# Splitting one chunk ahead of the mix, and both retention directions in one product: the output stage of a hybrid layer

## The chip, the cores and the metric

One NeuronCore of a Trainium2 chip runs the whole layer as one program. The metric is the device time of one execution in microseconds (us); several executions are timed and the median is given. One further execution is taken with the hardware profiler; all rows below are from that one.

## What is computed

The reference is one layer of a diffusion transformer on 2048 tokens of width 1024 (and 256 context tokens): a modulated RMS norm, a token mix, a residual, a second norm, and a mixture of 16 experts. The token mix has two halves of 512 columns, retention and RWKV-7, each run forward and backward over the sequence. For the retention half (8 heads of 64, chunks of 128 tokens) the part that matters here is

```python
def head_rms(y):
    y = y * lax.rsqrt(jnp.mean(y * y, axis=-1, keepdims=True) + NORM_EPS)
...
decay_in = where(rel >= 0, exp(max(rel, 0) * log_gamma), 0)
q_dec = exp((idx + 1) * log_gamma)
scores = einsum('bhid,bhjd->bhij', qc, kc) * decay_in
out = einsum('bhij,bhjd->bhid', scores, vc) + einsum('bhid,bhde->bhie', qc * q_dec, S)
S = S * chunk_dec + einsum('bhjd,bhje->bhde', kc * k_dec, vc)
...
lat = silu(gf) * head_rms(y_f) + silu(gb) * head_rms(flip(y_b))
...
lat = concatenate([ret_lat, rwkv_lat]) @ w_out
x = x + gt1 * rms_norm(mix, g_post_mix)
```

Then come the router's logits from the second norm of x, the choice of 256 tokens for each expert, and the experts.

## The kernel before, in words

Three earlier stages write projected columns, the retention states and the RWKV outputs to DRAM. `out_phase` (from L1375) is the output stage; it takes a chunk of 128 tokens at a time, 16 chunks, and ends with the router's logits; the experts follow. Its parts for one chunk are methods of `Chunk`:

- `turns`: load q and k, 8 TensorE transposes into two PSUM tiles `pb`, two ScalarE copies to `qT` and `kT`.
- `scores`: `qds` = qT times a table of decays `qd` for both directions (one GpSimd pass of 1024 columns); two `pb` tiles of k times q (4 matmuls each), each multiplied on VectorE by the decay mask `rm` into an `sm` tile of 1024 columns (both directions).
- `loads`, `gates`: DMA loads of v and gates (`vg`), the backward state (`Sb`), the RWKV outputs (`ys`), bonus (`bon`) and gates (`gs`); then three GpSimd passes on `gs` and `bon`.
- `wkv`: square, reduce, root, reciprocal and scale of `ys` (the head norm), then times `gs`, plus `bon`, into the right half of `lat`.
- `outputs(d)`, once for each direction: 16 small matmuls of `qds` with the state into PSUM tile `py`, 16 of `sm` with v on top, a ScalarE copy to `yr`, square, reduce; root, reciprocal, scale, times gate. The second direction adds both into the left half of `lat`.
- `split`: 8 transposes of `lat` into two `pb` tiles; ScalarE rounds each into `lh`, VectorE writes the rest into `ll`.
- `mix`: 48 matmuls of 512 columns (lh and ll with the split weights) into two PSUM tiles `pm`. `mixed`: squares and row sums of `pm` on ScalarE, `h` = `pm` times a gain row on VectorE, root and reciprocal.
- `norms`: x + norm (`xt<-h` in the rows, two instructions), its squares, root, `h` = the second norm (VectorE), plus a shift row (GpSimd); stores. `route`: 8 transposes of x into two `pb` tiles, copies to `hT`, 8 matmuls of 16 columns into a `pb` tile, logits.

The loop over i (L1652) interleaves these by hand. In the round of i it does the mix of chunk i, `norms` and `route` of chunk i-1, `outputs` and `wkv` of chunk i+1, `scores` of i+2 and `turns` of i+3, and `split` of i+1 near its end, ahead of the last 8 matmuls of the mix. TensorE, VectorE, ScalarE and GpSimd keep the program's order each (`keep_in_program_order`, L126, which is why all rows show L126); DMA issues on SyncE are put in order by a planner. At the head of a round stand, in this order: `gates`; squares and reduce of `wkv`; x and its squares; the second norm; root and scale of `wkv`. Then come five steps of 8 mix matmuls each with the other parts between them.

The stage divides PSUM into eight tiles of 512 columns (banks): three for tiles named `pb`, three for `pm`, two for `py`. A `pb` tile is free when its last reader is done.

Of the kernel before, what the change touches and what calls it, by code (L numbers as in the profile page):

```python
# [35 lines left out]
def constants():  # L36
# [28 lines left out]
    qd = lambda e: np.exp(e[None, None, :] * chan[:, :, None]) / 8  # L65
    c["ret_qdec"] = np.stack([qd(i + 1), qd(128 - i)], 1).reshape(128, 1024).astype(f)
# [18 lines left out]
def body(ctx: ExitStack, tc, a, out, scratch, stop=None, only=None):  # L85
# [1289 lines left out]
    def out_phase():  # L1375
        with ExitStack() as es:
# [12 lines left out]
            qd = one.tile([128, 2, 512], F32, name="qd")  # L1389
# [58 lines left out]
            def squares(x, n):  # L1448

                sq = one.tile([128, HD * n], F32, name="sq%d" % n)  # L1450
                act.activation(sq, x, AF.Square)
                ss = two.tile([128, n], F32, name="ss%d" % n)
                vec.tensor_reduce(ss, heads(sq), axis=AX.X, op=OP.add)
                return ss

            def head_norm(x, ss, n, eps):

                rstd(ss, 1.0 / HD, eps)
                vec.tensor_mul(heads(x), heads(x), ss[:, :, None].to_broadcast([128, n, HD]))
# [10 lines left out]
            Sf = one.tile([128, 4, HD], F32, name="Sf", bufs=3)  # L1470
            nc.sync.dma_start(out=Sf.rearrange("p s e -> p (s e)"), in_=g.kvf[16])
            Sf = advance(Sf, 17)

            class Chunk:
# [5 lines left out]
                def turns(self):  # L1480
# [3 lines left out]
                    for j, n in enumerate(("qT", "kT")):  # L1484
# [3 lines left out]
                        t = one.tile([128, 4, 128], F32, name=n)  # L1488
# [17 lines left out]
                def loads(self):  # L1506
# [3 lines left out]
                    Sb = two.tile([128, 4, HD], F32, name="Sb")  # L1510
                    nc.sync.dma_start(out=Sb.rearrange("p s e -> p (s e)"), in_=g.rb[self.i])
# [6 lines left out]
                    self.parts = (u, Sb, ys, bon, gs)  # L1518

                def outputs(self, d, Sf):  # L1520

                    u, Sb = self.parts[:2]
                    S = Sb if d else Sf
                    py = pps.tile([128, 2, 512], F32, name="py", bufs=1)
                    pyv = py[:, :, 0:256].rearrange("p z (s d) -> p z s d", d=HD)
# [8 lines left out]
                    for s in range(4):  # L1534
                        for hh in range(2):
                            for th in range(2):
                                mm(pyv[H[th], hh, s, :], self.sm[hh][:, d, s, ts[th]], u[:, hc(2 * s + hh)],
                                   start=False, stop=(s == 3), skip_group_check=True)
                    yr = one.tile([128, W], F32, name="yr", bufs=2)
                    act.copy(out=yr.rearrange("p (s z d) -> p z s d", z=2, d=HD), in_=pyv)  # L1540
# [4 lines left out]
                    if d == 0:  # L1545
                        self.y0 = yr
                    else:
                        vec.tensor_add(self.lat[:, 0:W], yr, self.y0)
# [10 lines left out]
                def wkv(self):  # L1559

                    _, _, ys, bon, gs = self.parts
                    self.lat = one.tile([128, D], F32, name="lat")
                    y = ys.rearrange("p d n -> p (d n)")
                    ss = squares(y, 16)
                    yield
                    head_norm(y, ss, 16, gn_eps)
                    yield
# [5 lines left out]
                def split(self):  # L1573
                    self.lh = lh = two.tile([128, KT, 128], F32R, name="lh")
                    self.ll = ll = two.tile([128, KT, 128], F32R, name="ll")
                    for j in (1, 0):
# [5 lines left out]
                        vec.tensor_sub(ll[:, js], ps, lh[:, js].bitcast(F32))  # L1582

# [66 lines left out]
            nc.sync.dma_start(out=qd.rearrange("p d n -> p (d n)"), in_=a["c_ret_qdec"])  # L1650
            nc.sync.dma_start(out=rm.rearrange("p d z s t -> p (d z s t)"), in_=a["c_ret_mask"])
            for i in range(-2, NT + 1):  # L1652
                if i == -1:
                    nc.sync.dma_start(out=lnw, in_=bcast(a["rwkv_lnx_w"], W))
                outs, other = [none, none], none
# [7 lines left out]
                if on(i + 1):  # L1663
                    ch[i + 1].gates()
# [499 lines left out]
```

## Time and profile before

| What | Value |
|---|---|
| Median of 3 runs | 3589.23 us (3582.62 to 3590.91) |
| The profiled execution: its own time, its span | 3576.91 us, 3574.9 us |
| TensorE, VectorE, ScalarE, GpSimd busy over the span | 89%, 64%, 39%, 34% |
| Mean granted TensorE clock over the span | 0.935 |
| The stretch of 12 rounds, 1919.7 to 2245.0 us: TensorE, VectorE, ScalarE, GpSimd busy | 285.2, 251.0, 121.9, 145.4 us of 325.3 |
| The same stretch: granted clock | 0.91 |
| Its start, 1848 to 1885.6 us (before the first mix): TensorE busy, clock | 19.8 us of 37.6, 0.50 |

Times of rows are us from the start of the span unless marked ns. PE is TensorE, DVE VectorE, ACT ScalarE, POOL GpSimd, SP SyncE. `out<-in` are the program's tile names; xN after a row is the number of instructions merged into it. Ends of matmuls are modelled, so the distance from one start to the next is the better price. A granted clock of 1.00 is 2.4 GHz, 0.50 is 1.2 GHz.

### The profile page before, as it was taken

To read this page: it belongs to the slowest core of one execution; us is meant where nothing else is said; L and a number is where in the kernel's file an instruction comes from. 1 tells how busy PE (TensorE), PEld (TensorE's weight loads), DVE (VectorE), ACT (ScalarE), POOL (GpSimd) and SP (SyncE) were. 2 spreads that over 40 slices of the span, in tenths; PEclk is the share of its full clock that TensorE was granted. 3 is DMA by queue.
4 is the path that set the end of the run, shared out by engine and by line. 5 is a ranking of instruction groups with operands and counts; after the bars stand their busy time and mean duration, and the time that the engine had idled before them with its cause. 6 is when DMAs were issued, how large, how long until landed. Compare 5 with 4: busy or idle time off the path is not lost. (4 is left out here: it accounts for less than half of the span.)

```text
span 3574.9 us, 74834 instructions
## 1 busy us (share of the span) xinstructions
PE 3197.0 (89%) x30786; PEld 2783.1 (78%) x30786; DVE 2271.5 (64%) x3904; ACT 1380.3 (39%) x2468; POOL 1216.9 (34%) x1969
## 2 busy tenths in 40 slices
PE   6999999788888888999978888849999999998888
PEld 4898889666767777777766777639999999998787
DVE  6676745566657556546427777675655665567765
ACT  4645343222222223333333333324444444444443
POOL 2010101464554554453634444220000000017774
PEclk9999999888999999999978988869999999999999
DMA  8886763545445456455457544236766666678885
GB/s 259 258 250 197 220 191 119 177 147 163 151 146 181 149 180 195 145 167 168 159 187 245 184 164 163 91 118 212 224 199 211 214 204 207 204 233 302 284 297 192
DMA packets 468221, 692.80 MB, mean 194 GB/s; under 512 B 30232, under 2 KB 345253, under 8 KB 457001
## 3 DMA queue, kind: packets, MB, share of 16 engines
q1 hardware_dynamic: 441480, 550.62, 47.4%
q0 software_dynamic: 25824, 136.36, 12.5%
q8 instruction: 242, 3.96, 0.4%
q10 hardware_dynamic: 576, 1.05, 0.1%
q14 instruction: 99, 0.80, 0.1%
HBM read 534.56 MB, written 153.37 MB: 192 GB/s over the span
## 5 line engine op out<-in xcount | busy, mean ns | idle before, releaser
L126 DVE TENSOR_TENSOR ewl<-ewr,ewh 128x1024 fp32r<-128x1024 f32 x376 | 474.3, 1303 | 250.2 <-ACT ewh L126 250.2
L126 PE MATMUL pr<-rwh,rh 128*128 128x512 f32 x1344 | 484.6, 428 | 35.7 <-ACT ru L126 16.9
L126 ACT CAST ewh<-ewr 128x1024 fp32r<-128x1024 f32 x376 | 374.2, 1046 | 0.5 <-DMA ewr<-in_w_down_dram 0.5
L126 PEld LDWEIGHTS pr<-rwh,rh 128*128 128x128 f32 x1344 | 268.7, 202 | 101.9 <-ACT ru L126 18.6
L126 PE MATMUL pu<-hi,whi 128*128 128x258 f32 (+1 forms) x1104 | 327.2, 296 | 5.0 <-ACT hi L406 5.0
L126 PE MATMUL pu<-lo,whi 128*128 128x258 f32 (+1 forms) x1104 | 315.9, 286 | 4.0 <-DVE lo L407 2.3
L126 PE MATMUL pu<-hi,wlo 128*128 128x258 f32 (+1 forms) x1104 | 314.4, 285 | 0.0
L997 POOL TENSOR_TENSOR dtmp<-xp,dm 128x126 f32<-128x126 f32 (+22 forms) x558 | 248.1, 445 | 186.8 <-DVE xp L126 146.9
L126 PE MATMUL pg<-xh,ewh 128*128 128x256 f32 x1024 | 293.0, 286 | 0.0
L126 PE MATMUL pu<-xh,ewh 128*128 128x256 f32 x1024 | 289.9, 283 | 0.8 <-DVE sg L126 0.8
L126 PE MATMUL pg<-xh,ewl 128*128 128x256 f32 x1024 | 290.4, 284 | 0.0
L126 PE MATMUL pg<-xl,ewh 128*128 128x256 f32 x1024 | 290.3, 284 | 0.0
L126 PE MATMUL pu<-xl,ewh 128*128 128x256 f32 x1024 | 289.9, 283 | 0.0
L126 PE MATMUL pu<-xh,ewl 128*128 128x256 f32 x1024 | 289.8, 283 | 0.0
L126 PE MATMUL pr<-rwl,rh 128*128 128x512 f32 x672 | 282.4, 420 | 4.4 <-DVE rwl L126 4.4
L1000 POOL TENSOR_TENSOR dm<-dm,dtmp 128x126 f32<-128x126 f32 (+22 forms) x558 | 269.0, 482 | 43.0
L126 PEld LDWEIGHTS pu<-hi,whi 128*128 128x128 f32 (+1 forms) x1104 | 208.2, 189 | 14.6 <-ACT hi L406 5.8
L126 PE MATMUL po<-ewh,hh 128*128 128x512 f32 x512 | 212.2, 414 | 0.0
L126 PEld LDWEIGHTS pu<-lo,whi 128*128 128x128 f32 (+1 forms) x1104 | 208.0, 188 | 5.2 <-DVE lo L407 3.2
L126 PEld LDWEIGHTS pu<-hi,wlo 128*128 128x128 f32 (+1 forms) x1104 | 208.6, 189 | 2.8 <-issue 2.2
L126 PE MATMUL po<-ewh,hl 128*128 128x512 f32 x512 | 203.6, 398 | 0.0
L126 PE MATMUL po<-ewl,hh 128*128 128x512 f32 x512 | 202.9, 396 | 0.0
(525 smaller groups left out, 7720.0 us busy)
## 6 DMA issues: line engine op xcount, KB each, us to landing
rh<-s_hT POOLq DMA_DIRECT2D x84, 1024.0 KB, 6.0
ewr<-in_w_gate_dram SPq DMA_DIRECT2D x64, 1024.0 KB
ewr<-in_w_up_dram SPq DMA_DIRECT2D x64, 1024.0 KB
ewr<-in_w_down_dram SPq DMA_DIRECT2D x64, 1024.0 KB
s_ret<-ru SPq DMA_DIRECT2D x84, 256.0 KB
wraw<-in_w_in_dram SPq DMA_DIRECT2D x156, 128.0 KB
bk<-s_bk SPq DMA_DIRECT2D x17, 1024.0 KB
mw<-in_w_mod_dram SPq DMA_DIRECT2D x128, 128.0 KB
```

The lines of the kernel that those rows point to most:

```text
L126: return lambda *args, **kw: tc.keep_in_program_order(op(*args, **kw))
L997: x = eng.tensor_mul(tv, ma[:, j, 0:j, None].to_broadcast(sh), dm[:, j:j + 1, j // 2:].to_broadcast(sh))
L1000: eng.tensor_add(dm[:, 0:j, j // 2:], dm[:, 0:j, j // 2:], tv)
```

## The change

- The decay of the queries is taken out of the product: the state is multiplied with plain `qT`, and the mask `rm` now holds decays relative to that, exp(-(j+1) log gamma) and its mirror, without the factor 1/8. The head norm divides the common factor out again, since it is the same for a whole row of a head; only the epsilon has to be scaled, and a table `ret_eps` (16 numbers a token, tile `reps`) is added to the sums of squares. `qds` and its table are gone, and `qT` gets a second buffer.
- Forward and backward state lie in one tile `S` (three buffers). `outputs` runs once for both directions: 16 matmuls of 128 columns instead of 2 x 16 of 64, the same 32 with `sm`, and then one square, reduce, root, reciprocal, scale and gating over 1024 columns instead of two each over 512.
- `outputs`, `wkv`, `gates` and `loads` work on chunk i+2 in the round of i, `scores` on i+3, `turns` on i+4. `split` stays with chunk i+1, and its two halves move from the end of the round to behind the first 8 and the second 8 mix matmuls. The loop begins at -3 instead of -2.

```diff
-    dec = lambda r: np.where(r[:, None, :] >= 0, np.exp(np.maximum(r, 0)[:, None, :] * lg[order][None, :, None]), 0) / 8
-    c["ret_mask"] = np.stack([dec(rel[:, :]), dec(-rel)], 1).reshape(128, 2048).astype(f)
+    dec = lambda r, e: np.where(r[:, None, :] >= 0, np.exp(-e[:, None, None] * lg[order][None, :, None]), 0)
+    c["ret_mask"] = np.stack([dec(rel, i + 1), dec(-rel, 128 - i)], 1).reshape(128, 2048).astype(f)
...
-    c["ret_qdec"] = np.stack([qd(i + 1), qd(128 - i)], 1).reshape(128, 1024).astype(f)
+    ep = lambda e: EPS * 64 * 64 * np.exp(-2 * e[:, None] * lg[None, :])
+    c["ret_eps"] = np.stack([ep(i + 1), ep(128 - i)], 1).reshape(128, 16).astype(f)
...
-                n = one.tile([128, 4, HD], F32, name="Sf", bufs=3)
-                pool.tensor_mul(n, S, cdec)
-                pool.tensor_add(n, n, f)
+                n = one.tile([128, 2, 4, HD], F32, name="S", bufs=3)
+                pool.tensor_mul(n[:, 0], S[:, 0], cdec)
+                pool.tensor_add(n[:, 0], n[:, 0], f)
...
-                    self.qds = two.tile([128, 2, 4, 128], F32, name="qds")
-                    pool.tensor_mul(self.qds.rearrange("p d s t -> p d (s t)"),
-                                         qT.rearrange("p s t -> p (s t)")[:, None, :].to_broadcast([128, 2, 512]), qd)
...
-                    nc.sync.dma_start(out=Sb.rearrange("p s e -> p (s e)"), in_=g.rb[self.i])
+                    nc.sync.dma_start(out=S[:, 1].rearrange("p s e -> p (s e)"), in_=g.rb[self.i])
...
-                py = pps.tile([128, 2, 512], F32, name="py", bufs=1)
+                py = pps.tile([128, 2, 4, 2, HD], F32, name="py", bufs=1)
...
-                            mm(pyv[H[th], hh, s, :], self.qds[H[hh], d, s, ts[th]], S[H[hh], s, :],
+                            mm(py[H[th], hh, s], self.T[0][H[hh], s, ts[th]], S[H[hh], :, s, :],
                                start=(s == 0), stop=False, skip_group_check=True)
                 yield
...
-                ss = squares(yr, 8)
+                    yr = one.tile([128, 2 * W], F32, name="yr")
+                    for hh in range(2):
+                        act.copy(out=yr.rearrange("p (d s z e) -> p z s d e", d=2, z=2, e=HD)[:, hh], in_=py[:, hh])
+                    ss = squares(yr, "r")
+                    vec.tensor_add(ss, ss, reps)
                     yield
-                head_norm(yr, ss, 8, eps1)
-                vec.tensor_mul(yr, yr, u[:, W + W * d:2 * W + W * d])
+                    head_norm(yr, ss)
+                    yield
+                    vec.tensor_mul(yr, yr, u[:, W:3 * W])
+                    vec.tensor_add(self.lat[:, 0:W], yr[:, 0:W], yr[:, W:2 * W])
...
-            for i in range(-2, NT + 1):
+            for i in range(-3, NT + 1):
...
-                if on(i + 1):
-                    ch[i + 1].loads()
-                    outs = [ch[i + 1].outputs(d, Sf) for d in range(2)]
-                    other = ch[i + 1].wkv()
+                if on(i + 2):
+                    ch[i + 2].loads(S)
+                    outs, other = ch[i + 2].outputs(), ch[i + 2].wkv()
+                split = ch[i + 1].split() if on(i + 1) else none
...
                     for _ in range(8):
                         next(mix, None)
+                    if step < 2:
+                        next(split, None)
                     if step < 4:
-                        next(outs[step // 2], None)
+                        next(outs, None)
                     if step == 1:
-                        if on(i + 2):
-                            ch[i + 2].scores()
-                        next(outs[0], None)
+                        if on(i + 3):
+                            ch[i + 3].scores()
                         next(other, None)
...
-                if on(i + 3):
-                    ch[i + 3].turns()
-                if on(i + 1):
-                    ch[i + 1].split()
+                if on(i + 4):
+                    ch[i + 4].turns()
                 for _ in range(8):
                     next(mix, None)
```

## Rows read from the trace of the kernel before

**Rows 1.** Instructions of tile h: duration ns min/median/max, first and last start.
```profile
L126 DVE SCALAR_TENSOR_TENSOR xt<-h,s__21977,xt x2: 742/744/746, 1919.7 to 1920.3; 128x512 f32<-128x512 f32 x2
...
L126 DVE SCALAR_TENSOR_TENSOR xt<-h,s__25133,xt x2: 743/744/746, 2245.0 to 2245.7; 128x512 f32<-128x512 f32 x2
...
L126 DVE SCALAR_TENSOR_TENSOR xt<-h,s__25606,xt x2: 747/750/753, 2296.9 to 2297.5; 128x512 f32<-128x512 f32 x2
L126 DVE SCALAR_TENSOR_TENSOR xt<-h,s__25716,xt x2: 746/749/752, 2314.2 to 2314.9; 128x512 f32<-128x512 f32 x2
```

**Rows 2.** Timeline of PE in one round: start, length, instruction, [idle before <-releaser].
```profile
2049.52 0.39 PE L126 MATMUL pm<-woh,lh 128*128 128x512 f32 x1
...
2051.48 0.70 PE L126 MATMUL py<-Sf,qds 64*64 64x64 f32 x32
...
2054.17 1.15 PE L126 MATMUL py<-vg,sm 128*64 128x64 f32 x32
2055.25 1.71 PE L126 MATMUL pb<-qT,kT 64*128 64x128 f32 x16
...
2070.66 1.12 PE L126 MATMUL pb<-ident,lat 128*128 128x128 f32 x4 [2.03 <-ACT qT L126]
2072.70 1.09 PE L126 MATMUL pb<-ident,lat 128*128 128x128 f32 x4 [0.91 <-DVE lat L126]
...
2076.65 0.39 PE L126 MATMUL pm<-woh,lh 128*128 128x512 f32 x1
```

**Rows 3.** PE by stretches: length, busy (instructions), granted clock, DMA share, GB/s.
```profile
2069.20:2076.20 7.00, 4.62 (x15) 0.51 0.92 325
```

**Rows 4.** Timeline of PE in the second round.
```profile
1919.21 0.69 PE L126 MATMUL py<-Sf,qds 64*64 64x64 f32 x32
...
1936.66 0.66 PE L126 MATMUL pb<-ident,lat 128*128 128x128 f32 x4 [0.65 <-ACT qT L126]
...
1938.69 0.63 PE L126 MATMUL pb<-ident,lat 128*128 128x128 f32 x4 [1.38 <-DVE lat L126]
...
1942.98 0.69 PE L126 MATMUL py<-Sf,qds 64*64 64x64 f32 x32
```

**Rows 5.** Timeline of DVE in the round of rows 2.
```profile
2050.49 0.69 DVE L126 TENSOR_TENSOR h<-pm,row_gt 128x512 f32<-128x512 f32 x1 [1.72 <-ACT junk L126]
...
2058.38 3.35 DVE L126 TENSOR_TENSOR ys<-ys,ss 128x1024 f32<-128x1024 f32 x1
...
2062.24 2.34 DVE L126 TENSOR_TENSOR sm<-pb,rm 128x1024 f32<-128x1024 f32 x2
...
2066.54 1.22 DVE L126 TENSOR_TENSOR ys<-ys,gs 128x1024 f32<-128x1024 f32 x1
...
2071.86 0.69 DVE L126 TENSOR_TENSOR lat<-yr 128x512 f32<-128x512 f32 x1
...
2072.61 0.68 DVE L126 TENSOR_TENSOR ll<-pb,lh 128x512 fp32r<-128x512 f32 x1
```

**Rows 6.** Timeline of POOL in the same round.
```profile
2058.26 2.38 POOL L126 TENSOR_TENSOR h<-h,row_sh 128x1024 f32<-128x1024 f32 x1 [7.86 <-DVE h L126]
2060.60 3.36 POOL L126 TENSOR_TENSOR qds<-qT,qd 128x1024 f32<-128x1024 f32 x1
...
2072.29 1.40 POOL L126 TENSOR_TENSOR both<-gs 128x512 f32<-128x512 f32 x1 [6.94 <-DMA gs<-s_g]
```

**Rows 7.** Timeline of ACT in the same round.
```profile
2051.49 1.04 ACT L126 ACTIVATE sq<-ys 128x1024 f32<-128x1024 f32 x1
```

**Rows 8.** Timeline of SP (DMA issues) in the same round.
```profile
2067.78 0.37 SPq L1517 DMA_DIRECT2D gs<-s_g  x1
```

**Rows 9.** Timeline of PE at the start of the stage.
```profile
1861.63 1.13 PE L126 MATMUL py<-Sf,qds 64*64 64x64 f32 x32
...
1880.58 1.09 PE L126 MATMUL pb<-ident,lat 128*128 128x128 f32 x4 [6.60 <-DVE lat L126]
...
1885.61 0.78 PE L126 MATMUL pm<-woh,lh 128*128 128x512 f32 x1
```

More of the change, by code (lines that the diff above doesn't have):

```diff
@@ L1388, in out_phase @@
             rm = one.tile([128, 2, 2, 4, 128], F32, name="rm")
-            qd = one.tile([128, 2, 512], F32, name="qd")
+            reps = one.tile([128, 16], F32, name="reps")
             rows = {n: one.tile([128, D], F32, name="row_" + n) for n in ("gt", "sh2", "sc2")}
@@ L1446, in out_phase, with squares, head_norm @@
             heads = lambda x: x.rearrange("p (h e) -> p h e", e=HD)
-            def squares(x, n):
-                sq = one.tile([128, HD * n], F32, name="sq%d" % n)
+            def squares(x, name):
+                sq = one.tile([128, 1024], F32, name="sq" + name)
                 act.activation(sq, x, AF.Square)
-                ss = two.tile([128, n], F32, name="ss%d" % n)
+                ss = two.tile([128, 16], F32, name="ss" + name)
                 vec.tensor_reduce(ss, heads(sq), axis=AX.X, op=OP.add)
                 return ss
-            def head_norm(x, ss, n, eps):
-                rstd(ss, 1.0 / HD, eps)
-                vec.tensor_mul(heads(x), heads(x), ss[:, :, None].to_broadcast([128, n, HD]))
+            def head_norm(x, ss, *eps):
+                act.activation(ss, ss, AF.Sqrt, scale=1.0 / HD, **(dict(bias=eps[0]) if eps else {}))
+                vec.reciprocal(ss, ss)
+                vec.tensor_mul(heads(x), heads(x), ss[:, :, None].to_broadcast([128, 16, HD]))
             def advance(S, i):
@@ L1464, in advance @@
                 nc.sync.dma_start(out=f.rearrange("p s e -> p (s e)"), in_=g.kvf[i])
[L1465 to L1472 removed]
+                n = one.tile([128, 2, 4, HD], F32, name="S", bufs=3)
+                pool.tensor_mul(n[:, 0], S[:, 0], cdec)
+                pool.tensor_add(n[:, 0], n[:, 0], f)
+                return n
+            S = one.tile([128, 2, 4, HD], F32, name="S", bufs=3)
+            nc.sync.dma_start(out=S[:, 0].rearrange("p s e -> p (s e)"), in_=g.kvf[16])
+            S = advance(S, 17)
             class Chunk:
@@ L1487, in turns @@
                             turn(ps[:, s, :], u[:, W * j + 128 * s:W * j + 128 * s + 128], ident)
-                        t = one.tile([128, 4, 128], F32, name=n)
+                        t = one.tile([128, 4, 128], F32, name=n, bufs=2 if j == 0 else 1)
                         act.copy(out=t, in_=ps)
@@ L1530, in outputs @@
                             for th in range(2):
-                                mm(pyv[H[th], hh, s, :], self.qds[H[hh], d, s, ts[th]], S[H[hh], s, :],
+                                mm(py[H[th], hh, s], self.T[0][H[hh], s, ts[th]], S[H[hh], :, s, :],
                                    start=(s == 0), stop=False, skip_group_check=True)
                     yield
[L1534 to L1540, printed above, removed]
-                    ss = squares(yr, 8)
-                    yield
-                    head_norm(yr, ss, 8, eps1)
-                    vec.tensor_mul(yr, yr, u[:, W + W * d:2 * W + W * d])
[L1545 to L1548, printed above, removed]
+                    for d in range(2):
+                        for s in range(4):
+                            for hh in range(2):
+                                for th in range(2):
+                                    mm(py[H[th], hh, s, d], self.sm[hh][:, d, s, ts[th]], u[:, hc(2 * s + hh)],
+                                       start=False, stop=(d == 1 and s == 3), skip_group_check=True)
+                        if d == 0:
+                            yield
+                    yr = one.tile([128, 2 * W], F32, name="yr")
+                    for hh in range(2):
+                        act.copy(out=yr.rearrange("p (d s z e) -> p z s d e", d=2, z=2, e=HD)[:, hh], in_=py[:, hh])
+                    ss = squares(yr, "r")
+                    vec.tensor_add(ss, ss, reps)
+                    yield
+                    head_norm(yr, ss)
+                    yield
+                    vec.tensor_mul(yr, yr, u[:, W:3 * W])
+                    vec.tensor_add(self.lat[:, 0:W], yr[:, 0:W], yr[:, W:2 * W])
                     yield
@@ L1662, in out_phase @@
                 norm = ch[i - 1].norms() if on(i - 1) else none
-                if on(i + 1):
-                    ch[i + 1].gates()
+                if on(i + 2):
+                    ch[i + 2].gates()
                 for part in (other, norm, norm, other) if i < NT else (norm, logit, norm):
@@ L1688, in out_phase @@
                         next(logit, None)
-                        next(outs[1], None)
-                        if on(i + 1) and on(i + 2):
-                            Sf = advance(Sf, i + 1)
+                        next(outs, None)
+                        if on(i + 2) and on(i + 3):
+                            S = advance(S, i + 2)
                 for _ in range(KT + 1):
                     next(logit, None)
-                if on(i + 3):
-                    ch[i + 3].turns()
-                if on(i + 1):
-                    ch[i + 1].split()
+                if on(i + 4):
+                    ch[i + 4].turns()
                 for _ in range(8):
```

29 lines of the change are left out of this document (13 added, 16 removed).

## Prediction

> **What bounds the kernel now.** I read the table of the profile first: TensorE has the largest share, but the change touches only the output stage, so the whole-span shares say little. The stage is 16 rounds, and the twelve full ones give its pace: the first row of a round's x falls at 1919.7, the thirteenth at 2245.0, so 325.3 / 12 = 27.1 us a round [rows 1]. The next view is TensorE's timeline in one round, to see what it waits for [rows 2]. Two waits stand out, both ahead of the transposes of `lat`: 2.03 us put down to the ScalarE copy of q, and 0.91 us to VectorE's `lat`. Behind them the granted clock is 0.51, the 1.2 GHz level, for 7.0 us, 4.6 of them busy [rows 3]. At the 2.4 GHz level that work takes 2.3 us less. So a round loses about 3 us of waiting and 2.3 us of clock. Its work without either is read from the second round: 1942.98 - 1919.21 = 23.77, less waits of 0.65 and 1.38, gives 21.7 us, with no fall of the clock after those two waits [rows 4].
>
> What makes TensorE wait is VectorE: the left half of `lat` is written last, at 2071.86, 22.3 us into a round that begins (first mix matmul) at 2049.52 [rows 2, 5]. I call that beginning T0. All times below with a plus sign count from T0.
>
> **The change, part by part.** *Split moved.* Transposes of `lat` now come one round after `lat` is written, so both waits at the end of the round go: -2.9 us, and with them the cause of the clock's fall there.
>
> But the moved step issues more than transposes. Each half also puts a rounding copy on ScalarE and a subtraction `ll` on VectorE, and the `pb` bank of that half is free only after `ll`. There are three `pb` banks. In the new order TensorE asks for four before it can do without one back: split half one, split half two, first scores, second scores. The second scores must wait for the first `ll`. And on VectorE that first `ll` now stands behind the head of the round: the gain product `h` at +1.0, x, the second norm, and the scale of `ys`, which runs from 2058.38 for 3.35 us, to +12.2 [rows 5]. None of these can start earlier, since x needs the whole mix of the round before. Why the scale takes 3.35 us where a pass of the same size takes 1.22 is seen on GpSimd: the shift of `h` runs 2058.26 to 2060.64, and VectorE's pass ends 1.1 us after that [rows 5, 6]. The removed `qds` comes behind both, so its removal does not bring this forward. With `ll` at 0.68 [rows 5] the bank is back at +12.9.
>
> TensorE reaches the second scores much earlier: 8 mix 1.96, half a split about 0.55 (four transposes take 1.09 at half clock), state product 0.9, 8 mix 1.96, half a split 0.55, the forward `sm` product 1.08, first scores 0.85 (half of 1.71) [rows 2]: +7.85. **So a wait of 5.05 us takes the place of the two of 2.9.** Behind the second scores TensorE has queued the backward `sm` product, four groups of the mix, the router's and q's transposes; VectorE's second `sm` pass waits for them too, and the next round's head for the end of the mix. The transfer of the backward state, which now goes into a tile that `advance` makes only a few steps earlier, and the price of the state product stand before this wait and cost nothing as long as they take less than 5 us more.
>
> Perfetto Trace Analysis in the Trainium skill, section Matmuls, asks that independent matmul groups rotate through different PSUM banks so that reading one out overlaps with the next group. Taken as fulfilled by three banks it would give the round of the rival without a wait, 22.5 us; the order of the `ll` on VectorE gives the wait of 5 us instead, and no row of before shows this order.
>
> *State product.* 2 x 0.70 become one of 16 matmuls with twice the columns. Below, the price per instruction: 0.70; above, the price per column: 1.40 [rows 2]. I take 0.9, so TensorE's work falls by 0.5 to 21.2 us, of which 21.2 - 7.85 = 13.4 lie behind the second scores' start.
>
> *`qds` gone:* 3.36 us of GpSimd [rows 6], off the path. *Norm and gating as one:* VectorE saves a reduce's and a reciprocal's fixed part and adds the small sum with `reps`, under 1 us; it stands in the tail of the round, which decides only if it comes too late (below).
>
> *The round.* +12.9 until the bank is back, then 13.4 of work: 26.3 us with the clock at full. Clock: at present the fall begins 0.6 us into the wait (2069.2 against 2070.66 - 2.03 = 2068.63) and lasts 7.0 us [rows 2, 3]. If it does the same at the new wait, 4.45 of the 7.0 are idle, 2.55 busy, and 1.3 us are lost. Bounds: 0, as in the second round [rows 4], and 2.3, as now [rows 3]. Tail: `sm` products behind the scores end at +12.9 + 0.85 + 1.96 + 1.08 and some 1.2 of slow clock, +18.0; three ScalarE passes at 1.04 for 1024 columns and about half for each copy [rows 7], +20.1; reduce, root, reciprocal and three passes at 1.22, 1.22 and 0.69 [rows 5], about 5.1, +25.2. Meanwhile `gs` of the next chunk is free when `ys` times `gs` ends: `ll` twice, `sm` twice (1.17 each, the second after the late scores), 1.22: about +17.0. Its load is issued then, and the first GpSimd pass `both` follows 4.5 us behind the issue (2067.78 to 2072.29) [rows 6, 8], at +21.5. Its three passes, 1.4, about 1.4 and 2.4, then meet the two-operand passes of VectorE's tail, and as with `h` and `ys` one waits for the other. VectorE's tail then ends 3 to 4 us later, near +28.5; the gain products should begin at T0' + 0.3, T0' being +27.6. So 0 to 1.6 us late; I take 0.6. Round: 12.9 + 13.4 + 1.3 + 0.6 = 28.2 us, against 27.1: +1.1.
>
> *Ends.* Twelve rounds like this: +13.2, less 1.0 for one that now lacks the transposes of q. The two rounds behind them take 51.9 us now (2245.0 to 2296.9) [rows 1]; the first then has no scores, so no such wait: 21.2 less 1.7 and 1.0 of scores and q, plus some 3 of waiting for copies of x behind the root, plus 1 of clock, 22.5; the second has no outputs and is like the last one now, 17.3 (2296.9 to 2314.2). That is -12.1. At the start, one more chunk's outputs, scores and q-transposes stand ahead of the first mix at 1885.61, and all runs at half clock there: by the 1.13 of a state product [rows 9], about 10 us of TensorE work in all; but 6.6 us of waiting for `lat` [rows 9] are there to take some of it. Between 0 and 10, I take 6.
>
> Sum: 13.2 - 1.0 - 12.1 + 6 = +6 us. The profiled execution took 3576.9, so 3583 of its kind; it lies 12.3 below the median of the runs, so 3595 as a median. A difference under 0.2%, 7 us, is about what this measurement cannot tell from no change.
>
> **The rivals.** The round at which nothing is won or lost is 27.1 + 7.1 / 12 = 27.7 us.
>
> *The period stays* at 27.1 to 27.4: the clock costs 1 us and the tail nothing. For it: the present 27.1 already holds waits of 2.9 and lost clock of 2.3 [rows 2, 3], and the new terms come close to their sum. -7 to -3 us: 3584.
>
> *The clock does not fall*: one long wait instead of two short ones, with dense work on both sides, and the tail early enough. Round 26.3 to 26.9, faster: 12 x -0.8 - 7 = -17 at best, 3572 to 3580. Against it: shorter waits bring the fall now. It decides where clock and tail cost less than 0.8 us together.
>
> *The change does what it says*: no wait at all. The round would be TensorE's 21.2 plus a little, some 22.5, since VectorE is busy 251.0 / 12 = 20.9 (the table): -62 us, 3527. Only if the scores found a bank without `ll`.
>
> *The tail collides*: GpSimd's three passes stand in front of the gating, the root that ScalarE takes for it also holds back the copies of x to `hT`, and both the router's matmuls and the gain products come late: 1.6 instead of 0.6, clock at 1.7. Round 29.2 to 29.6: +18 to +23, 3607 to 3612. It decides from about 1.5 us of lateness on.
>
> **How the numbers follow.** Forecast (round 27.7 to 28.8, 0 to +13 us): 0.42. Period stays: 0.20. Clock stays up: 0.16. No wait: 0.05. Tail collides: 0.17. The likeliest gives 3595, its own range 3589 to 3602. Left out of 3574 to 3611 are the no-wait case, a third of the clock case and a third of the collision. Slower by over 0.2%: the collision and a bit under half of the forecast, 0.36. Faster: no wait, most of the clock case, a little of the unchanged one, 0.24. Within: 0.40.
>
> **What would show it.** In a full round: transposes of `lat` without a wait; the only long idle time of TensorE, 4 to 6 us, between the two halves of the scores (`pb<-qT,kT`), released by VectorE's `ll`; that `ll` about 12 us after the round's first mix matmul, straight behind the `ys` pass of 3.35 us; a granted clock of 0.5 behind that idle time for 2 to 3 busy us. The rows of x 28.2 us apart. `both` about 4 us behind `ys<-ys,gs`, and gating passes of VectorE well over 1.22 us. The first mix about 6 us later than 1885.6. The prediction is wrong if the scores are not held up by `ll`, or if the rounds are 27 us or shorter.

## Result and profile after

The changed kernel takes 3607.93 us in the median of 4 runs (3604.99 to 3612.45), the kernel before 3590.07 beside it (3582.62 to 3591.73): 17.9 us more, a ratio of 1.006 with a 95% interval of 1.0044 to 1.0076. The forecast was 3595, 6 us more, with a range of 3574 to 3611. The direction and the range were right, the size was too small by a factor of three.

The rows of x give the pace again [rows 1]. In the profile after, instructions of tile h (first and last start):

```profile
L128 DVE SCALAR_TENSOR_TENSOR xt<-h,s__22040,xt x2: 744/745/746, 1930.9 to 1931.6; 128x512 f32<-128x512 f32 x2
...
L128 DVE SCALAR_TENSOR_TENSOR xt<-h,s__24844,xt x2: 743/744/746, 2286.9 to 2287.6; 128x512 f32<-128x512 f32 x2
...
L128 DVE SCALAR_TENSOR_TENSOR xt<-h,s__25268,xt x2: 746/749/752, 2344.5 to 2345.1; 128x512 f32<-128x512 f32 x2
```

Twelve rounds take 2286.9 - 1930.9 = 356.0 us, 29.67 each, against 27.11. Both kernels were profiled a second time, each in one further execution, since the first profile of before (3576.91) lay under its median. The same rows there, before first, then after:

```profile
L126 DVE SCALAR_TENSOR_TENSOR xt<-h,s__21977,xt x2: 745/745/745, 1928.9 to 1929.5; 128x512 f32<-128x512 f32 x2
...
L126 DVE SCALAR_TENSOR_TENSOR xt<-h,s__25133,xt x2: 742/743/744, 2260.6 to 2261.2; 128x512 f32<-128x512 f32 x2
```

```profile
L128 DVE SCALAR_TENSOR_TENSOR xt<-h,s__22040,xt x2: 744/746/747, 1938.2 to 1938.9; 128x512 f32<-128x512 f32 x2
...
L128 DVE SCALAR_TENSOR_TENSOR xt<-h,s__24844,xt x2: 743/743/743, 2288.3 to 2288.9; 128x512 f32<-128x512 f32 x2
```

That is 331.7 / 12 = 27.64 before and 350.1 / 12 = 29.18 after. So a round costs 1.5 to 2.6 us more, depending on the pair, and an execution of one kernel differs from the next by half a microsecond a round.

| Term, us | forecast | first pair | second pair |
|---|---|---|---|
| first row of x later | +6 | +11.2 | +9.3 |
| twelve rounds | +12.2 | +30.7 | +18.4 |
| the rest of the stage | -12.1 | -11.6 | -11.6 |
| sum | +6 | +30.3 | +16.1 |
| whole executions | | 3604.99 - 3576.91 = +28.1 | 3607.59 - 3592.91 = +14.7 |

The round without the transposes of q, -1.0 in the forecast, is the last of the twelve, so it is counted with them.

TensorE in one of the usual rounds after (timeline: start, length, instruction, idle time before it and its releaser), the counterpart of [rows 2]:

```profile
2047.48 0.39 PE L128 MATMUL pm<-woh,lh 128*128 128x512 f32 x1
...
2049.32 0.60 PE L128 MATMUL pb<-ident,lat 128*128 128x128 f32 x4
2049.85 1.10 PE L128 MATMUL py<-S,qT 64*64 64x128 f32 x32
...
2054.47 1.16 PE L128 MATMUL pb<-qT,kT 64*128 64x128 f32 x8
2060.30 2.07 PE L128 MATMUL pb<-qT,kT 64*128 64x128 f32 x8 [4.68 <-DVE ll L128]
...
2076.66 0.39 PE L128 MATMUL pm<-woh,lh 128*128 128x512 f32 x1
```

The transposes of `lat` no longer wait. The one long wait is at the second `scores`, released by `ll`, 12.8 us after the round's first mix matmul. VectorE shows why it is so late (timeline; rows that answer to [rows 5]):

```profile
2048.47 0.69 DVE L128 TENSOR_TENSOR h<-pm,row_gt 128x512 f32<-128x512 f32 x1 [0.62 <-ACT junk L128]
...
2056.34 3.30 DVE L128 TENSOR_TENSOR ys<-ys,ssw 128x1024 f32<-128x1024 f32 x1
2059.57 1.27 DVE L128 TENSOR_TENSOR ll<-pb,lh 128x512 fp32r<-128x512 f32 x2
```

`ll` stands straight behind the scale of `ys`, which again takes 3.3 us beside GpSimd's shift. Now the clock around that wait (stretches of TensorE: length, busy time and instructions, granted clock, DMA share, GB/s), to be laid beside [rows 3]:

```profile
2055.60:2059.90 4.30, 0.02 (x1) 0.99 0.19 71
2059.90:2066.30 6.40, 6.00 (x22) 0.50 0.28 81
```

TensorE idles for 4.3 us at a clock that still reads 0.99. The clock falls when the wait is nearly over, to 0.50, the 1.2 GHz level, and stays there for 6.4 us of which 6.0 are busy: 3.0 us lost. In the kernel before, the fall began 0.6 us into a shorter wait and 4.6 of its 7.0 us were busy [rows 3].

For all runs below I cut the twelve rounds into stretches of 0.2 us. "Lost" is busy time times one minus the granted clock, "work" is what is left of the busy time, so it is TensorE's work at full clock.

| Kernel | ratio to before (95%) | round | work | idle | lost |
|---|---|---|---|---|---|
| before, two profiles | 1 | 27.11, 27.64 | 21.9, 21.8 | 3.35, 3.49 | 1.87, 2.36 |
| after, two profiles | 1.006 (1.0044 to 1.0076) | 29.67, 29.18 | 21.5, 21.5 | 5.09, 4.79 | 3.05, 2.86 |
| four banks | 1.0001 (0.9989 to 1.0013) | 28.17 | 21.0 | 3.47 | 3.68 |
| scores ahead of split | 0.9841 (0.9818 to 0.9864) | 24.06 | 21.3 | 2.33 | 0.41 |
| wait filled | 1.0008 (0.9993 to 1.0024) | 28.02 | 26.7 | 1.03 | 0.29 |
| fusing alone | 1.0023 (1.0011 to 1.0036) | 28.16 | 21.3 | 3.19 | 3.65 |
| copies first | 1.0016 (1.0004 to 1.0029) | 29.00 | 21.3 | 4.65 | 3.04 |
| fusing alone, copies first | 1.0018 (1.0003 to 1.0033) | 28.25 | 21.4 | 4.63 | 2.27 |
| four banks, copies first | 0.9924 (0.9903 to 0.9946) | 25.83 | 21.0 | 3.26 | 1.53 |
| scores ahead, four banks | 0.9878 (0.9858 to 0.9898) | 24.77 | 21.7 | 2.46 | 0.66 |
| shift on VectorE | 1.0048 (1.0031 to 1.0065) | 29.59 | 21.5 | 4.89 | 3.22 |
| copies first, shift on VectorE | 1.0014 (1.0001 to 1.0027) | 28.70 | 21.3 | 4.42 | 2.96 |
| scores ahead, shift on VectorE | 0.9838 (0.9821 to 0.9854) | 24.37 | 21.3 | 2.12 | 0.93 |

The ratios stand against runs of before on the same chip, whose medians were 3590.07 us for the changed kernel and 3583.9 to 3586.0 us for the others. The other columns come from one profiled execution each, so a difference of less than half a microsecond a round between two kernels says little. One of the ten executions of the fusing alone with copies first took 12619 us and is left out of its ratio.

### The profile page after: what moved, and what is told of

Read it like the earlier page. It is cut to its first block, busy times and chain, and to the rows that moved or that the text cites. A ratio compares the mean times of both kernels' runs of the same rounds, so it can differ in the third digit from the quotient of the medians.

```text
span 3603.0 us, 73720 instructions
## 1 busy us (share of the span) xinstructions
PE 3204.6 (89%) x30274; PEld 2793.6 (78%) x30274; DVE 2282.6 (63%) x3856; ACT 1371.2 (38%) x2436; POOL 1181.2 (33%) x1953
```

## Experiments

The theory: the round is set by a `pb` bank that only VectorE's `ll` frees, plus the clock that is lost behind that wait. The rivals: VectorE's chain sets the round whatever the banks are; or the fusing itself costs the time, by the place of the norm.

**Second profiles.** No edit; they gave the figures of the second pair above.

> The kernel before once more, for a second profile. The first profiled execution took 3576.9 us with rounds of 27.1 us, some 12 below the median of its runs. If the stage varies from one execution to the next, the rounds are 27.3 to 28 us here with more clock lost than 1.87 us a round; if the difference lies outside the stage, the rounds are 27.1 again.

> The changed kernel once more, for a second profile. If its first profile is typical, the rounds are 29.5 to 29.8 us again with 5 us idle and 3 us of clock lost in each; if the clock falls by chance, rounds of 29.0 to 29.4 with 2 to 2.6 us lost.

Before: 27.64 us a round and 2.36 lost, so the stage itself varies between executions. After: 29.18, below the 29.5 to 29.8 of "typical", and 2.86 lost, above the 2.0 to 2.6 of the other case. What differs between the two profiles of after are long rounds of 30.5 us and more: four of twelve in the first, one in the second. Behind all four of the first there is more clock lost, 3.4 to 4.0 us.

**Four banks.**

```diff
-  ps = pps.tile([128, 4, 128], F32, name="pb", bufs=3)
+  ps = pps.tile([128, 4, 128], F32, name="pb", bufs=4)
...
-  pm = pps.tile([128, 512], F32, name="pm", bufs=3)
+  pm = pps.tile([128, 512], F32, name="pm", bufs=2)
```

> One bank moves from the mix's pm ring (3 to 2) to the pb ring (3 to 4), all else as in the changed kernel. Theory (the second scores wait for a bank that only the first ll frees): the second scores start right behind the first ones, and the 4.7 us of waiting there go; some come back at the next limit (copies of hT behind the root on ScalarE, the sm passes behind the ll on VectorE), so a round of 26 to 27.5 us instead of 29.7 and 25 to 45 us less in all. Rival (VectorE's chain from the head of the round to the hT copies sets the round, and the bank's wait only shows where TensorE spends its spare time): the wait moves to the sm products or the hT transposes, the round stays within 0.5 of 29.7, the time within 8 us of the changed kernel. A second rival: with two pm banks the mix itself now waits for the gain product of the round before, which shows as a wait at the mix's first matmul.

The round fell to 28.17, and the wait at the scores was gone. TensorE's waits from 1950 to 2240 us (total, times, longest) have this in its place, and under it ScalarE's timeline in one round:

```profile
PE pb L128 <- ACT hT L128: 37.3, 10, 3.8
```

```profile
2072.39 1.06 ACT L128 ACTIVATE sqr<-yr 128x1024 f32<-128x1024 f32 x1
2078.80 0.22 ACT L128 ACTIVATE ssr<-ssr 128x16 f32<-128x16 f32 x1 [5.35 <-DVE ssr L128]
2078.92 1.05 ACT L128 COPY hT<-pb 128x512 f32<-128x512 f32 x2
```

ScalarE does nothing for 5.35 us in front of the root `ssr`, which waits for VectorE's reduce, and the copies of x to `hT` that the router needs are queued behind it. So there are two limits that hid each other: with three banks 4.7 us at the scores, with four 3.7 us at the router. The theory's mechanism held; its 26 to 27.5 did not, since I had not priced that second one.

**Copies first.** In the kernel before, the copies to `hT` stood ahead of the second direction's root; the change put the only root ahead of them.

```diff
+                    if step == 3:
+                        next(logit, None)
                     if step < 4:
                         next(outs, None)
...
                     if step == 3:
-                        next(logit, None)
                         next(outs, None)
```

> The changed kernel, with the router's transposes of x and their two copies to hT put ahead of the root of the head norm on ScalarE (in the kernel before they stood ahead of the second direction's root); the wait of the second scores for ll's bank stays. Theory (the bank is the first limit, the root's place the second): the wait of some 0.5 us a round at the router's matmuls goes and with it part of the second fall of the clock, the bank's wait stays at 4 to 5 us: round 28.7 to 29.4 against 29.7, 3 to 12 us less. Rival (the root's place is the real cost): round 27 or less, 30 us less. Rival: nothing, within 3 us.

29.00 us, no wait for `hT`, and the bank's wait unchanged (1950 to 2200 us):

```profile
PE pb L128 <- DVE ll L128: 38.3, 8, 5.3
```

The rounds are now all of 28.3 to 29.6, so the long ones of after (30.5 to 31.4) hung on the root's place. But 3.04 us of clock are still lost: the second fall was not the larger part. The time fell more than expected, by a ratio of 1.006 to 1.0016, some 16 us: about 8 in the twelve rounds against the first profile (2 against the second), 6 in the last three, which went from 57.6 to 51.6 us, the rest within what executions differ by.

**Both at once.** The two diffs above together.

> The changed kernel with both of its waits taken away: four pb banks and two pm banks, and the copies to hT ahead of the root. Theory (bank and root are two waits in a row, each hidden by the other when one alone is taken away: the four banks gave 1.5 us a round and a wait of 3.5 us at the router in its place): neither wait is left, the clock stays up, the round is set by VectorE's chain at 24 to 25.5 us, 55 to 70 us less than the changed kernel, about as fast as the scores put ahead of the split. Rival (VectorE's tail is late in any case): the wait shows at the mix's end or as TensorE waiting for a pm bank, round 27 to 28, no more than 10 us less than the four banks alone.

25.83 us, in ten rounds out of twelve 25.7 or 25.8; neither wait is left. It is short of the 24 to 25.5 expected and 27 us below before (0.9924). What holds it up shows in VectorE's timeline, in one round:

```profile
2074.80 2.25 DVE L128 TENSOR_TENSOR yr<-yr,vg 128x1024 f32<-128x1024 f32 x1
2077.08 1.65 DVE L128 TENSOR_TENSOR lat<-yr 128x512 f32<-128x512 f32 x1
```

and in TensorE's waits (1950 to 2200 us): it now stands at the mix, for a `pm` bank that the gain product `h` frees.

```profile
PE pm L128 <- DVE h L128: 31.5, 9, 4.7
```

Two passes of 1.22 and 0.69 us take 2.25 and 1.65 beside GpSimd's passes for the next gates: 2.0 us a round on the engine that TensorE now waits for. That the mix has only two `pm` banks here is part of this wait; no run has four `pb` and three `pm`. The lost clock costs this round nothing that shows: from the third on the rounds lost between 0.0 and 2.7 us each, and all took 25.7 or 25.8.

**Scores ahead of the split.** The order of the requests is changed instead of the number of banks.

```diff
-                    if step < 2:
+                    if step in (2, 3):
                         next(split, None)
...
                     if step == 1:
...
-                        next(other, None)
                         next(norm, None)
...
                     if step == 3:
                         next(logit, None)
+                        next(other, None)
                         next(outs, None)
```

> The two halves of the split go from steps 0 and 1 of the mix to steps 2 and 3, behind both scores, and the last part of the wkv side goes from step 1 to step 3 so that it still follows the split. Then the scores find banks freed by ScalarE's copies of q and k, and ll is the last reader of a bank that is asked for only by the router and the turns. Theory (order of the banks' requests sets the wait): no wait at the scores, clock up through the mix, round 23 to 25 us, 55 to 75 us less than the changed kernel, so some 35 to 55 us below the kernel before. Rival (VectorE, busy 21 us a round, sets a chain of its own): the scale of ys and the ll come late at step 3, the wait comes back at the hT transposes or the router, round 27 to 28, 15 to 30 us less than the changed kernel. If the wait is only moved in full: round 29 to 30.

24.06 us a round and 0.9841: the best of all, 57 us below before. TensorE in one round, and that round's stretch:

```profile
2065.21 1.71 PE L128 MATMUL pb<-qT,kT 64*128 64x128 f32 x16
...
2074.43 0.66 PE L128 MATMUL pb<-ident,lat 128*128 128x128 f32 x4 [1.90 <-DVE sm L128]
2075.56 1.25 PE L128 MATMUL pb<-ident,xt 128*128 128x128 f32 x8 [0.47 <-DVE sm L128]
```

```profile
2063.90:2087.80 23.90, 21.53 (x202) 1.00 0.52 188
```

Both scores run in one piece, and the time fell by more than the 55 to 75 us expected. What is left is 2.4 us of waiting for banks that the `sm` passes hold, and in nine of the twelve rounds the clock did not fall. The last part of the wkv side, `ys` times `gs`, also moved, and with it the issue of the next gates' load: GpSimd's passes no longer meet VectorE's gating, which takes 1.22 and 0.69 again:

```profile
2081.95 1.22 DVE L128 TENSOR_TENSOR yr<-yr,vg 128x1024 f32<-128x1024 f32 x1
2083.21 0.69 DVE L128 TENSOR_TENSOR lat<-yr 128x512 f32<-128x512 f32 x1
```

They meet x instead, one of whose two passes takes 1.76 us instead of 0.74. The run does not separate this part from the order of the banks. With the root still ahead of the copies, TensorE waits for `hT` once between 1950 and 2240 us, 0.7 us: the price of the root's place depended on the queue in front of VectorE's reduce.

**Scores ahead, four banks.** The diffs of the two together.

> The split behind the scores, with four pb banks and two pm banks. With three banks it has a round of 24.06 and waits of 2.8 us a round at the second half of the split and at the transposes of x for banks that VectorE's sm passes hold. Theory (VectorE is the next limit: busy some 20.5 us of a round of 24, and its idle time lies in the norm's chain with ScalarE): the waits shrink but the round only goes to 23 to 23.8, 3 to 12 us less. Rival (TensorE is the limit through the bank): the 2.3 idle us go, round 21.8 to 22.5, 18 to 27 us less. Rival: two pm banks make the mix wait for the gain product, round 24.3 to 26.

24.77, slower than three banks (0.9878 against 0.9841). The last rival came true; the wait at the `sm` banks shrank from 2.4 to 0.8 us a round and this came in its place (1950 to 2200 us):

```profile
PE pm L128 <- DVE h L128: 15.3, 10, 1.8
```

The eight banks are all used (`py` holds two), so each bank is taken from a ring that needs it.

**Wait filled.** Twenty matmuls of zeros on an open accumulator between the two scores; they add zero and leave nothing out (`fill` is the first `pm` tile of chunk i, `zr` a tile of zeros).

```diff
+                        if hh and fill is not None:
+                            for _ in range(20):
+                                mm(fill, zr, wh[:, 0, 0:512], start=False, stop=False, skip_group_check=True)
```

> In each full round 20 matmuls of a zero tile (512 columns each, added to an open accumulator, so they add zero) stand between the two halves of the scores, where TensorE waits 4.7 us; nothing else changes. They fill about 4.4 us at full clock. Theory (3.05 us of a round are lost because the clock falls behind idle time): the granted clock stays up behind the wait, loss of 1 us or less a round, round about 27.5 to 28.2, 18 to 28 us less than the changed kernel although TensorE does more. Rival (the chain behind the second scores runs on VectorE, not on TensorE, so its clock doesn't matter): the clock stays up, but the round stays at 29.2 to 29.7. Second rival: the fill itself runs at the low level or ends after the bank is free, round 30 to 33.

One round in TensorE's timeline, and the same round as a stretch:

```profile
2072.26 1.16 PE L128 MATMUL pb<-qT,kT 64*128 64x128 f32 x8
2073.34 4.93 PE L128 MATMUL pm<-woh,zr 128*128 128x512 f32 x20
2078.20 1.16 PE L128 MATMUL pb<-qT,kT 64*128 64x128 f32 x8
...
2091.55 0.39 PE L128 MATMUL pm<-woh,lh 128*128 128x512 f32 x1
```

```profile
2069.40:2097.70 28.30, 28.30 (x239) 1.00 0.48 158
```

The clock stays up: 0.29 us lost a round instead of 3.05. From the second scores to the next round's first mix it is 2091.55 - 2078.20 = 13.35 us, against 2076.66 - 2060.30 = 16.36 in the kernel after: the 3.0 us of lost clock are time of TensorE's chain behind the wait, not hidden behind VectorE. But not all of them reach the round. Against the first profile of after, work rises by 26.70 - 21.53 = 5.17, idle time falls by 4.06 and lost clock by 2.76, and the round is 1.65 shorter (1.16 against the second profile). What is missing shows in TensorE's waits from 1950 to 2240 us: in most rounds `ll` now comes behind the fill, and the router waits for `hT`.

```profile
PE pb L128 <- DVE ll L128: 6.9, 8, 1.9
PE pb L128 <- ACT hT L128: 4.3, 7, 0.8
```

So the round and the time (0.52% less than after) came as the theory said, but only about half of the clock that was won back shortened the round.

**Fusing alone.** All steps back at their places of before; the product, the table, the one norm and the one gating kept (`for i in range(-2, ...)`, outputs and loads on i+1, scores on i+2, turns on i+3, split behind the router).

> Only the fusing is left of the change: one state product for both directions, the eps table in place of the decayed queries, one norm and one gating; the split, the scores, the turns and the outputs stand at the places of the kernel before (split behind the router, in the same round as lat). Theory (the fusing is a small gain and the moved split alone costs): no wait at the scores, the waits ahead of the transposes of lat as before or up to 1 us longer, since lat's left half is now written after both directions instead of after the second one; round 26 to 27.3, so 0 to 15 us below the kernel before. Rival (the fusing itself puts the whole norm at the end of the round, in front of lat): the wait ahead of the transposes of lat grows by 1.5 to 3 us, round 28.5 to 30, 15 to 35 us slower than the kernel before.

28.16 us and 1.0023: the fusing on its own is 8 us slower than before, where the theory had it up to 15 us faster. The result is closer to the rival's, but the wait stands at the router and not at `lat`. And with the copies first:

> The kernel with the fusing alone (all steps at the places of before) and the copies to hT ahead of the root. With the fusing alone the router's matmuls waited 3.3 us a round for copies behind the root, and lat was ready just as TensorE came to it, without a wait. Theory (the fused norm ends late because both directions now go through VectorE in one piece at the end of the round, and the root's place only shows it first): the wait moves from the router to the transposes of lat, 3 to 4.5 us there, round 27.7 to 28.3, within 6 us of the fusing alone. Rival (the root's place alone costs it): no wait of over 1.5 us at lat, round 25.5 to 26.7, 15 to 30 us less than the fusing alone.

28.25 and 1.0018, unchanged, as the theory said: the wait only moved. The fusing alone, then with the copies first, in TensorE's timeline:

```profile
2077.51 3.59 PE L128 MATMUL pb<-wr,hT 128*128 128x16 f32 x16 [3.27 <-ACT hT L128]
```

```profile
2077.09 1.08 PE L128 MATMUL pb<-ident,lat 128*128 128x128 f32 x4 [4.38 <-DVE lat L128]
```

Both directions go through VectorE in one piece behind the second `sm` product, so `lat` is ready late, and with the split in the same round TensorE waits 3.3 us at the router or 4.4 at `lat` for it.

**Shift on VectorE.** A test of how exactly the queue in front of `ll` counts.

```diff
-                    pool.tensor_add(t, t, rows["sh2"])
+                    vec.tensor_add(t, t, rows["sh2"])
```

> The changed kernel with the shift of h (a sum with a row) on VectorE instead of GpSimd, nothing else. There it should take about 1.22 us as the other passes of that size, and the scale of ys behind it 1.22 instead of 3.3, since GpSimd's shift no longer runs beside it: VectorE reaches the first ll about 0.9 us earlier. Theory (the bank is freed when VectorE's queue reaches ll, so each microsecond in front of ll is one of the round): the second scores wait 3.7 to 4.0 us instead of 4.7, the round is 28.5 to 29.0 instead of 29.7, 9 to 16 us less than the changed kernel. Rival (ll waits for something else, or the next limit takes over at once): the wait or the round stays, within 4 us of the changed kernel.

The scale of `ys` went to 1.22 us and the wait to 3.9 to 4.3 in the plain rounds of 28.1 to 28.8 (from the third round on), so `ll` came 0.4 to 0.8 us earlier. But the other six rounds took 29.4 to 33.4, and the mean was 29.59: a miss. In the longest, VectorE, GpSimd and TensorE show what happens:

```profile
2036.92 2.04 DVE L128 TENSOR_TENSOR ssr<-ssr,reps 128x16 f32<-128x16 f32 x1
```

```profile
2036.55 2.38 POOL L128 TENSOR_TENSOR gs<-gs,lnw 128x1024 f32<-128x1024 f32 x1
```

```profile
2039.74 3.20 PE L128 MATMUL pb<-wr,hT 128*128 128x16 f32 x16 [1.55 <-ACT hT L128]
```

The sum with `reps`, 16 numbers a row and 0.17 to 0.18 us where it is alone, ends with GpSimd's pass, 2.0 us after its start. The root waits for it, the copies to `hT` for the root, the router for them, and the clock falls a second time in the round (6.8 us lost in this one). So I ran the shift with the copies first, too:

> The copies to hT ahead of the root and the shift of h on VectorE, both at once. The shift on VectorE alone brought ll some 0.7 us earlier and cut the wait of the second scores to 4.3 us, but 5 of 12 rounds were long (30.5 to 33.4 us), with the small sum with reps taking up to 2 us beside a GpSimd pass, the root and the copies to hT late behind it and the clock falling a second time; its plain rounds were 28.1 to 28.8. With the copies first the root holds nothing up. Theory (each microsecond in front of ll is one of the round, and the long rounds hung on the root's place): all rounds 28.0 to 28.7, 4 to 12 us less than the copies first alone (29.0 us a round). Rival (what ll gains, the rest of the round loses): rounds of 28.9 to 29.2 on average, or long rounds again.

All rounds are 28.1 to 29.1, mean 28.70: the long ones are gone, and 0.3 us is gained on the copies first, less than two executions of one kernel differ by. The mean is the upper end of the theory's range, and single rounds lie above it. The wait is 4.3 to 4.4 us where the gain products start 0.8 to 0.95 us behind the round's first mix matmul, and 4.7 to 5.2 us where VectorE's tail holds them until +1.25 to +1.7, in about every second round: what the shorter queue gives is partly given back at the head of the round. The time is that of the copies first (1.0014 and 1.0016). That each microsecond in front of `ll` is a whole one of the round is not shown.

**Scores ahead, shift on VectorE.**

> The split behind the scores, and the shift of h on VectorE as well. The split behind the scores had a round of 24.06 us, with 2.8 us of waiting for banks that the sm passes hold, and the sm passes stand behind the same scale of ys. Theory: sm comes 0.9 us earlier, the waits at the banks shrink by as much, round 23.1 to 23.6, 5 to 12 us less than the split behind the scores. Rival (GpSimd's other passes meet VectorE's work elsewhere, as at x, where two passes took 2.4 instead of 1.4 us): nothing or a loss, 24 to 24.6.

24.37 and 0.9838, no difference to the scores ahead alone. The wait at the `sm` banks went from 2.4 to 2.2 us a round, while the passes around the shift took 1.5 instead of 1.2 to 1.3 beside GpSimd's other work: the rival.

## Why the prediction was off

**The place and the cause of the wait were right.** A second `scores` behind `ll`, the bank back at +12.9 (measured 2060.30 - 2047.48 = 12.8), a wait of 5.05 (4.68), in place of the two at `lat`. Four banks and the other order each removed it, as the argument of three banks and four requests says. The rule of the Trainium skill (Perfetto Trace Analysis, Matmuls) on rotating banks is not contradicted: with four banks in rotation the wait went; with three, the order of what is read out decides.

**The work behind the wait was right.** From the second scores' start to the next round it is 16.36 us, less 3.0 of lost clock 13.4, as forecast. The state product took 1.03 us (from its start at 2049.85 to the next at 2050.88), inside its bounds and 0.13 over the value taken.

**The clock term failed.** I wrote "if it does the same at the new wait": the fall begins 0.6 us into the wait, 4.45 of its 7.0 us are idle, 1.3 are lost. It did not do the same. It came 4.3 us into the wait, and nearly all of the slow stretch was work: 2.86 to 3.05 lost, above the bound of 2.3, which was only what before lost. That is 1.6 to 1.75 us a round, 19 to 21 us over twelve, more than the 11.9 us by which the medians miss the forecast. The run with the wait filled shows these 3 us as time behind the second scores, 16.36 against 13.35; without them the round was 1.2 to 1.65 us shorter.

**The tail was taken half wrong.** In the usual round the gain products are not late (2048.47 is +1.0), so the 0.6 us is not there; the round is 28.2 + 1.7 - 0.6 = 29.3 by this, against 29.0 to 29.2. The rival "the tail collides" named the root that holds back the copies to `hT`. It did so: between 1950 and 2240 us TensorE waits for `hT` 6.4 us in the first profile of after and 2.3 in the second, 0.6 and 0.2 a round, in the first most of it in the long rounds. Its time, 3607 to 3612, is the one that was measured, but that is half luck: its clock of 1.7 was too small as well, and its lateness of 1.6 too large. Sum with `reps` and GpSimd, as in the run with the shift, in the profile after (all rounds: min, median, max in ns):

```profile
L128 DVE TENSOR_TENSOR ssr<-ssr,reps x16: 174/854/2204, 1876.2 to 2299.9; 128x16 f32<-128x16 f32 x16
```

I had put this new instruction and the saved parts of the fused norm together at under 1 us, in the tail of the round; it stands on the path of the root. The Trainium skill says of VectorE and GpSimd (Trainium Architecture — The Big Picture, What this means for kernel authors) that they share a port pair under an exclusive lock, not a split bandwidth. The rows agree: 0.18 us alone, up to 2.2 beside a pass of GpSimd.

**The start left out round 0**: +6 against +9.3 and +11.2. The 6 us were put on the first mix, which came 3.4 us later in the first pair (1889.00 against 1885.61 [rows 9]) and 7.5 in the second (1897.70 against 1890.16). The round behind it had no term in the sum. It grew by 7.8 and 1.8 (in the second profile of before it was itself 4.6 us longer), since it has the new wait too, beside one for `lat`, and part of it at the low clock: half of the scores take 2.07 us there instead of 1.16 (TensorE's timeline, first profile):

```profile
1889.00 0.48 PE L128 MATMUL pm<-woh,lh 128*128 128x512 f32 x1
...
1898.68 0.63 PE L128 MATMUL pb<-ident,lat 128*128 128x128 f32 x4 [3.32 <-DVE lat L128]
...
1907.07 2.07 PE L128 MATMUL pb<-qT,kT 64*128 64x128 f32 x8 [3.92 <-DVE ll L128]
```

**The ends** were forecast at -12.1 and came to -11.6. The 3 us of copies behind the root that I had put there were seen: 2.73 us of waiting for `hT` in the first round behind the twelve; with the copies first the last three rounds take 6 us less.

**Where the gain went.** Fusing makes `lat` late (+8 us by itself); moving the split one round ahead takes `lat` off the path, but asks for a bank that `ll` holds, and the clock falls behind that wait. No run moves the split without the fusing, so the price of the moved split alone is read only as the difference of the two. With the scores ahead of the split the fused kernel is 1.6% faster than before: that was the "no wait" rival, given 0.05, with 22.5 us a round; it came to 24.06 there.

Open: the first and second profile of a kernel differ by 0.5 us a round. Part of it are the long rounds of after; why before differs by as much, and why the clock falls early in one wait and late in another, these runs do not tell.

## What to carry to other kernels

When a step with its own buffers moves, list the requests for the ring in the new order and ask for each which queue its last reader stands in; the cheap repair is the order (here the split behind the scores, with the end of the wkv side moved along: -80 us against the changed kernel), not one more bank. Two waits in a row hide each other, so removing one alone says little: test both and the pair. Price a long wait with the lost clock on the work behind it (here 3 us behind 4.7), but count it in the round only where TensorE's own chain sets it (filling the wait gave back 1.2 to 1.65 us, and with both waits gone the clock cost nothing that showed). Price fused passes by when their result is ready, not by their summed length.

## What was unexpected of the hardware

- The granted clock held at 0.99 through 4.3 us of idle time and fell as the work came back; in the kernel before it fell 0.6 us into a 2.0 us wait. With the scores ahead of the split, 2.4 us of waiting a round, it stayed at 1.00 in nine of twelve rounds.
- A 128x16 sum on VectorE took 0.17 to 0.18 us alone and up to 2.2 us beside a GpSimd pass, ending with that pass.
- The state product of 32 matmuls on 64x64 quadrants with 128 columns took 1.10 us (1.03 to the next start), against 0.70 for 64 columns [rows 2]: about halfway between a price by instruction (0.70) and one by column (1.40).
